# Moving the layer-input projection of an encoder block from its last stage to the end of its mixer

## The chip, the cores and the metric

The kernel runs on one core of a Trainium2 chip. The metric is the device time of one execution, in microseconds (us). Before the change it is 963.14 us, the median of three runs (962.81 to 963.81). About 0.2% of it, 1.9 us, can be told from no change.

A core has five engines, each with its own queue of instructions that it takes in order: TensorE (PE in the profile) for matmuls, with its weight loads shown apart (PEld); VectorE (DVE); ScalarE (ACT); GpSimd (POOL); and SyncE (SP), which here only issues DMAs. SBUF holds the working tiles of 128 partitions, PSUM the results of matmuls in eight banks.

## The reference, cut to what matters

One layer, 512 frames of width 1024, all in float32. `_swiglu`, `_conv_module` and `_gla` are the usual ones: a gated feed-forward block, a causal depthwise convolution of width 31 with layer norm over 512 channels, and a gated linear attention with four heads.

```
h = x
h = h + 0.5 * _swiglu(_rmsnorm(h, ffn1_norm[i]), ffn1_w_in[i], ffn1_w_out[i])
z = _rmsnorm(h, mix_norm[i]) @ w_in[i]
conv_a, conv_gt, q, k, v, r, g_lr = jnp.split(z, SPLIT_POINTS, axis=-1)
y_conv = _conv_module(conv_a, conv_gt, conv_w[i], conv_b[i], conv_ln_g[i], conv_ln_b[i])
y_gla = _gla(q, k, v, r, g_lr, gate_w_up[i], gate_b[i], gla_norm[i])
h = h + jnp.concatenate([y_conv, y_gla], axis=-1) @ w_out[i]
h = h + 0.5 * _swiglu(_rmsnorm(h, ffn2_norm[i]), ffn2_w_in[i], ffn2_w_out[i])
gate = jax.nn.sigmoid(_rmsnorm(h, ple_norm[i]) @ ple_w_gate[i])
h = h + gate * (p[i] @ ple_w_proj[i])
return _rmsnorm(h, final_norm)
```

The projection of the title is `p[i] @ ple_w_proj[i]`: p is 512 x 256, the weight 256 x 1024. It depends on nothing that the layer computes.

## The kernel before

**Precision.** A float32 product is made of three matmuls: each operand is split into a rounded high part and the low rest, and high x high, high x low and low x high are added in PSUM (`mm3`, line 209). The high part is a copy on ScalarE (`high`, line 183, and `high4`, line 219, which puts a weight into four smaller tiles), the low part a subtraction on VectorE (`low`, line 193). `added` (line 198) makes the low part otherwise: ScalarE writes the negated weight, and a DMA issued by GpSimd adds the weight to it. `ahead` (line 214) has GpSimd do the subtractions.

**Tiles.** `bt` hands out 41 tiles of 128 x 512 (tag A), `raw` six buffers for loaded weights, the tags wh and wl six each for their parts, `tmp("u1")` two, `bank` seven PSUM banks and `aux` one. An instruction that needs a tile waits until one is free.

**Order.** `Ordered` (lines 36 to 60) chains the instructions of PE, DVE and ACT in the order of the program text, from `in_order(True)` to `in_order(False)` at line 1446; this is why nearly every instruction is recorded under line 46. POOL and SP are not chained: the framework queues them by its own model of when each can start. In the last stage no engine is chained.

**Stages.** The first feed-forward block (up to about 363 us in the profile) is driven by a list of units with due times (`drive`, line 575): weights are fetched and split a fixed number of units ahead, and hooks run behind named units. Its last cut of the output product is done in pieces (`second`, line 742): first and second halves of four output pairs. The hook ("m4", 10) loads four tiles of the input projection and splits them at once (line 875).

The mixer follows. `zblock` (line 233) makes 128 x 512 blocks of the input projection, `tokblock` (line 1089) blocks of 128 tokens for v and r. The convolution is 124 VectorE steps, 31 for each of four channel groups, that `taps(n)` (line 905) puts between other work, always from the first two unfinished groups in turn; a call that finds a group finished is spent on removing it. `rsqrt_mean` (line 243) makes a root with a power on GpSimd, `spread` and `colsum` are small matmuls.

In the mixer's end (lines 1249 to 1416) the four blocks of r are made, gated with the attention's output (`ytok`), transposed into `yps`, split into `mix[4..7]` (ygH, ygL), and multiplied with the lower half of each of the eight output weights (`first_part`, line 1244). Between these stand four matmuls with a constant matrix (`mean`) that sum the convolution's four groups; then come the layer norm's squares, its root (`ln_sums`, a hook inside the half block of weight 3), its spreading and the norm itself (`ln_out`, a hook inside the half block of weight 6), which give `mix[0..3]` (ycH, ycL). The upper halves of the output weights follow, for weights 0 to 2 together, then one by one (`wout_h`, line 1361, takes each result into h).

The second feed-forward block is like the first (to about 894 us); `turn_p` (line 1395), which transposes and splits p, is hooked into its last units. In the last stage (lines 1451 to 1520), for each half e of the width and each token block t, six matmuls make the projection, ScalarE copies it out, four transposes bring h back to tokens, 24 matmuls make the gate, and `gated` combines them; the second half also normalises and stores.

Of the kernel before, what the change touches and what calls it, by code (L numbers as in the profile page):

```python
# [15 lines left out]
P = 128  # L16
SEQ = 512
# [45 lines left out]
def block_kernel(ctx: ExitStack, tc: tile.TileContext, a: dict, out: bass.AP):  # L63
# [11 lines left out]
    tp = ctx.enter_context(tc.tile_pool(name="tmp", bufs=2))  # L75
    pp = ctx.enter_context(tc.tile_pool(name="ps", bufs=8, space=PSUM))
# [137 lines left out]
    def ahead(src, c0, ncol):  # L214


        return [[low(w, pool) for w in high4(load(src, 0, DC, c, P))] for c in range(c0, c0 + ncol, P)]
# [377 lines left out]
    def ffn(w_in, w_out, x, gname, given, first, rsb, hooks, plain):  # L595
# [146 lines left out]
        def second(cut):  # L742
# [62 lines left out]
            if not last:  # L805
                return [piece(n, 0, True, True, ("g2", f0) if n == 0 else None) for n in range(0, DC, 2)]
            return ([piece(n, 0, True, False) for n in range(0, 6, 2)],
                    [piece(n, 1, False, True) for n in range(0, 6, 2)] + [piece(6, 0, True, False),
# [54 lines left out]
    w_ahead = []  # L863

    def sums_hooks(x, names, at):

        h = {}
        for name, key in zip(names, at):
# [6 lines left out]
                  ("m4", 10): lambda *_: w_ahead.extend([ahead(w_in, D_CONV, 2 * P), ahead(w_in, 0, 2 * P)])})  # L875
# [15 lines left out]
    glu, acc, conv = [], [cvt() for _ in range(4)], []  # L891
# [11 lines left out]
    turn = [0]  # L903

    def taps(n):

        for _ in range(n):
            if not conv:
                return
            i = turn[0] % min(2, len(conv))  # L910
            turn[0] += 1
            try:
                next(conv[i])
            except StopIteration:
                conv.pop(i)
# [13 lines left out]
    def glu_out(a1, sg):  # L929
# [3 lines left out]
        conv.append(conv_steps(len(glu) - 1))  # L933
# [33 lines left out]
    wq = [high(raw_q[0])]  # L967
    taps(2)
    low(wq[0])
    taps(1)  # L970
# [11 lines left out]
    wq.append(high(raw_q[1]))  # L982
# [24 lines left out]
    wk = [high(raw_k[0])]  # L1007
    low(wq[1])
    raw_v = [load(w_in, k, 2, C_V, SEQ) for k in (0, 2)]
    cums, epos, eneg, edec, decay, ends = [], [], [], [], [], []  # L1010
    taps(8)
    glu_out(glu_value(pa), sg)
    pb = zblock(w2b[1], hg)
    taps(3)
    low(wk[0])
# [18 lines left out]
    wk.append(high(raw_k[1]))  # L1034
# [29 lines left out]
    low(wk[1])  # L1064
# [3 lines left out]
    taps(5)  # L1068
# [181 lines left out]
    wo, rt = {n: added(ohigh(n)) for n in (0, 1)}, []  # L1250
    for t in range(TB):
# [5 lines left out]
        elif t == 1:  # L1257
            ps = tokblock(wr, t, {2: lambda: outputs(1)})
            taps(15)
# [7 lines left out]
        else:  # L1267
            ps = tokblock(wr, t)
# [14 lines left out]
        if t > 0:  # L1283
            taps((0, 2, 5, 3)[t])
# [3 lines left out]
    mub = aux()  # L1288
    for t in range(TB):
        if t == 2:  # L1290
            for c in range(2):
                pe.matmul(mub, mean, acc[c], start=(c == 0), stop=False)
        for h in range(4):
            pe.transpose(yps[h][:, t * P:(t + 1) * P], ytok[t][:, h * HV:(h + 1) * HV], ident)
    taps(2)
# [3 lines left out]
    wo[3] = ohigh(3)  # L1299
# [3 lines left out]
    pbt = [bt(s="ptok") for _ in range(2)]  # L1303
    ptok = [pbt[t // 2][:, (t % 2) * D_PLE:(t % 2 + 1) * D_PLE] for t in range(TB)]
# [4 lines left out]
    for steps in list(conv):  # L1309
        for _ in steps:  # L1310
            pass
# [232 lines left out]
```

## Time and profile before

| | |
|---|---|
| runs | 963.81, 962.81, 963.14 us |
| profiled execution | 963.15 us, its span from first to last instruction 961.4 us |
| instructions | 14302 |
| TensorE clock granted | 0.999 |
| VectorE, ScalarE, GpSimd busy | 72%, 52%, 4% of the span |
| DMA | 99.15 MB, mean 103 GB/s |

Times are microseconds from the start of the span. "Waits" list, for an engine, the tile that it was about to write or read, who released it, the total, the number of times and the longest. A timeline row is a start, a duration, the engine, and what is written from what; several like instructions in a row are merged (x4), and idle time before the row stands behind it with its releaser. The chain of waits is the chain of work that ended last. A stretch (busy time by windows) has the pairs PE, PEld, DVE, ACT, POOL as busy time and count, then the granted clock, the DMA share and GB/s.

### The profile page before, as it was taken

How to read it: one execution, taken by the hardware profiler on the slowest of the kernel's cores; microseconds unless marked ns; L12 is line 12 of the kernel's file. 1: busy time of each engine (PE TensorE's matmuls, PEld its weight loads, DVE VectorE, ACT ScalarE, POOL GpSimd, SP SyncE). 2: the span in 40 equal slices, each digit the busy share in tenths (PEclk: the TensorE clock that was granted, in tenths of full speed). 3: DMA queues.
4: the chain of work that ended last, by engine and by line, in shares of the span. 5: the costliest groups of instructions: out<-in, count | busy, mean ns of one | idle time of the engine just before them, and what ended most of it. 6: DMA issues, size and time to landing. Idle time of an engine off the chain costs nothing.

```text
span 961.4 us, 14302 instructions
## 1 busy us (share of the span) xinstructions
PE 947.4 (99%) x5809; PEld 838.4 (87%) x5809; DVE 693.6 (72%) x912; ACT 504.4 (52%) x795; POOL 38.8 (4%) x49
## 2 busy tenths in 40 slices
PE   8999999999999999999999999999999999999996
PEld 7888999999999978788877888999999999998885
DVE  4885767677677585999987679866776766767554
ACT  4854655554554453463564646556545555546442
POOL 0000000000000310001120000000000000000000
PEclk9999999999999999999999999999999999999999
DMA  8441323343223561125543232432243223334102
GB/s 244 140 130 64 104 72 112 109 131 93 84 88 110 153 175 50 39 85 136 132 96 102 75 101 66 132 98 80 88 132 110 82 92 113 96 125 153 45 1 88
DMA packets 102854, 99.15 MB, mean 103 GB/s; under 512 B 4499, under 2 KB 95717, under 8 KB 102788
## 3 DMA queue, kind: packets, MB, share of 16 engines
q1 hardware_dynamic: 100916, 94.05, 31.9%
q0 software_dynamic: 1296, 3.67, 2.2%
q8 instruction: 45, 0.74, 0.3%
q10 hardware_dynamic: 576, 0.52, 0.2%
q14 instruction: 21, 0.17, 0.1%
HBM read 92.46 MB, written 2.10 MB: 98 GB/s over the span
## 4 chain that ended last, share of the span: by engine, by line
PE 95%; DMA 1%; DVE 1%; ACT 1%; issue 1%; POOL 0%; SPq 0%; POOLq 0%; DVEq 0%; ACTq 0%
PE ps L46 94%; PE ax L46 1%; DMA wr<-in_w_in 1%; DMA x<-in_x 0%; DVE wl L46 0%; ACT wh L46 0%; POOL wa L46 0%; ACT wa L46 0%; DVE g L46 0%; ACT yc L46 0%; DVE ygL L46 0%; DVE actL L46 0%; DVE yc L46 0%; ACT ygH L46 0%; POOLq L1540 0%
## 5 line engine op out<-in xcount | busy, mean ns | idle before, releaser
L46 DVE TENSOR_TENSOR wl<-wr,wh 128x1024 fp32r<-128x1024 f32 (+2 forms) x181 | 214.3, 1195 | 76.1 <-ACT wh L46 75.7
L46 PE MATMUL ps<-hgH,wh 128*128 128x256 f32 (+1 forms) x768 | 239.6, 317 | 0.0
L46 PE MATMUL ps<-hgH,wl 128*128 128x256 f32 (+1 forms) x768 | 238.0, 315 | 0.0
L46 PE MATMUL ps<-hgL,wh 128*128 128x256 f32 (+1 forms) x768 | 237.9, 315 | 0.0
L46 ACT CAST wh<-wr 128x1024 fp32r<-128x1024 f32 (+2 forms) x186 | 187.4, 1024 | 40.0 <-PE ps L46 20.2
L46 PEld LDWEIGHTS ps<-hgH,wh 128*128 128x128 f32 x768 | 146.3, 191 | 11.7 <-ACT hgH L46 2.0
L46 PEld LDWEIGHTS ps<-hgL,wh 128*128 128x128 f32 x768 | 147.0, 191 | 9.8
L46 PEld LDWEIGHTS ps<-hgH,wl 128*128 128x128 f32 x768 | 145.9, 191 | 8.3
L46 PE MATMUL ps<-actH,wh 128*128 128x512 f32 x352 | 137.6, 391 | 1.2 <-ACT actH L46 1.2
L46 PE MATMUL ps<-actL,wh 128*128 128x512 f32 x352 | 137.5, 391 | 0.2 <-DVE actL L46 0.2
L46 PE MATMUL ps<-actH,wl 128*128 128x512 f32 x352 | 137.0, 389 | 0.0
L46 ACT ACTIVATE h<-ps 128x512 f32<-128x512 f32 x64 | 38.1, 595 | 115.1 <-PE ps L46 115.1
L46 DVE SCALAR_TENSOR_TENSOR cv<-glu,cw,cv 128x504 f32<-128x504 f32 (+25 forms) x120 | 81.2, 729 | 0.6
L46 PEld LDWEIGHTS ps<-actH,wh 128*128 128x128 f32 x352 | 66.2, 188 | 14.5 <-ACT actH L46 1.6
L46 ACT ACTIVATE s<-g 128x512 f32<-128x512 f32 x48 | 30.2, 629 | 91.4 <-DVE g L46 91.4
L46 PEld LDWEIGHTS ps<-actH,wl 128*128 128x128 f32 x352 | 66.1, 188 | 13.9
L46 PEld LDWEIGHTS ps<-actL,wh 128*128 128x128 f32 x352 | 66.2, 188 | 13.1 <-DVE actL L46 0.5
L46 DVE TENSOR_TENSOR actL<-m,actH 128x512 fp32r<-128x512 f32 x44 | 28.7, 689 | 43.1 <-ACT actH L46 42.9
L46 PE MATMUL ps<-wh,hgH 128*128 128x512 f32 (+1 forms) x136 | 52.4, 385 | 0.0
L46 PE MATMUL ps<-wl,hgH 128*128 128x512 f32 (+1 forms) x136 | 51.7, 380 | 0.0
L46 PE MATMUL ps<-wh,hgL 128*128 128x512 f32 (+1 forms) x136 | 51.3, 377 | 0.0
L46 DVE TENSOR_TENSOR wl<-sm,wh 128x1024 fp32r<-128x1024 f32 x34 | 41.4, 1218 | 10.1 <-ACT wh L46 10.1
(227 smaller groups left out, 1618.4 us busy)
## 6 DMA issues: line engine op xcount, KB each, us to landing
wr<-in_ffn_w_in SPq DMA_DIRECT2D x84, 512.0 KB
wr<-in_ffn_w_out SPq DMA_DIRECT2D x32, 512.0 KB
wr<-in_w_in SPq DMA_DIRECT2D x20, 512.0 KB
wr<-in_ffn_w_out SPq DMA_DIRECT2D x16, 384.0 KB
wr<-in_w_out SPq DMA_DIRECT2D x8, 512.0 KB
wr<-in_ple_w_gate SPq DMA_DIRECT2D x8, 512.0 KB
wl<-wr POOLq DMA_DIRECT2D x5, 512.0 KB, 5.6
x<-in_x SPq DMA_DIRECT2D x8, 256.0 KB
```

Source lines behind the costliest of these rows:

```text
L46: inst = call(*args, **kwargs)
```

## The change

The projection's eight groups (two halves of the width, four token blocks) are made in the mixer's end by a new function `project` and stored to a DRAM tile; the last stage loads each group back into the tile where ScalarE's copy went before. The tokens of p are loaded, transposed (inside the third r block) and split in the mixer, and the projection's weight is split into tag-A tiles with `added`. Two groups stand ahead of the first half block, one behind the third, three behind the layer norm's column sums, two behind its spreading.

The four mean products become one, over the sum of the four groups that VectorE makes; the half blocks of weights 3, 6 and 7 are done after the joint loop of weights 0 to 2, in the order 0, 1, 2, 4, 5, 3, 6, 7, and these three weights are split after the layer norm.

`taps` now takes the group with the most steps left, never the same one twice in a row if another is ready, and no call is spent on removal. The weights of q and k are split with `added`, with more convolution steps in place of the subtractions. The four tiles of the input projection that were split at once behind ("m4", 10) are now only loaded there; they are split behind two pieces of the output product (new keys ("p", 4) and ("p", 0)).

The diff, cut to its changed lines:

```diff
@@ -73,6 +73,7 @@
+    dp = ctx.enter_context(tc.tile_pool(name="spill", bufs=1, space=bass.MemoryType.DRAM))
@@ -211,10 +212,9 @@
-    def ahead(src, c0, ncol):
-        return [[low(w, pool) for w in high4(load(src, 0, DC, c, P))] for c in range(c0, c0 + ncol, P)]
+    def ahead(raws):
+        return [[low(w, pool) for w in high4(r3)] for r3 in raws]
@@ -804,8 +804,8 @@
-            return ([piece(n, 0, True, False) for n in range(0, 6, 2)],
-                    [piece(n, 1, False, True) for n in range(0, 6, 2)] + [piece(6, 0, True, False),
+            return ([piece(n, 0, True, False, ("p", n) if n else None) for n in range(0, 6, 2)],
+                    [piece(n, 1, False, True, None if n else ("p", n)) for n in range(0, 6, 2)] + [piece(6, 0, True, False),
@@ -860,7 +860,7 @@
-    w_ahead = []
+    w_ahead, raw_ahead = [], []
@@ -872,7 +872,9 @@
-                  ("m4", 10): lambda *_: w_ahead.extend([ahead(w_in, D_CONV, 2 * P), ahead(w_in, 0, 2 * P)])})
+                  ("m4", 10): lambda *_: raw_ahead.extend(load(w_in, 0, DC, c, P) for c in (D_CONV, D_CONV + P, 0, P)),
+                  ("p", 4): lambda *_: w_ahead.append(ahead(raw_ahead[:2])),
+                  ("p", 0): lambda *_: w_ahead.append(ahead(raw_ahead[2:]))})
@@ -888,7 +890,7 @@
-    glu, acc, conv = [], [cvt() for _ in range(4)], []
+    glu, acc, conv, steps_of = [], [cvt() for _ in range(4)], [], {}
@@ -900,19 +902,20 @@
-    turn = [0]
+    left = {}
...
-            i = turn[0] % min(2, len(conv))
-            turn[0] += 1
-            try:
-                next(conv[i])
-            except StopIteration:
-                conv.pop(i)
+            ready = conv[:2] if len(glu) < 4 or len(conv) > 3 else conv
+            c = max((c for c in ready if c != left.get("last") or len(ready) == 1), key=lambda c: left[c])
+            next(steps_of[c])
+            left["last"] = c
+            left[c] -= 1
+            if not left[c]:
+                conv.remove(c)
@@ -930,7 +933,9 @@
-        conv.append(conv_steps(len(glu) - 1))
+        c = len(glu) - 1
+        conv.append(c)
+        left[c], steps_of[c] = PAD + 1, conv_steps(c)
@@ -964,10 +969,8 @@
-    wq = [high(raw_q[0])]
-    taps(2)
-    low(wq[0])
-    taps(1)
+    wq = [added(high(raw_q[0]))]
+    taps(4)
@@ -979,7 +982,7 @@
-    wq.append(high(raw_q[1]))
+    wq.append(added(high(raw_q[1])))
@@ -1004,15 +1007,13 @@
-    wk = [high(raw_k[0])]
-    low(wq[1])
+    wk = [added(high(raw_k[0]))]
...
-    taps(8)
+    taps(10)
...
-    taps(3)
-    low(wk[0])
+    taps(5)
@@ -1031,7 +1032,7 @@
-    wk.append(high(raw_k[1]))
+    wk.append(added(high(raw_k[1])))
@@ -1061,11 +1062,10 @@
-    low(wk[1])
...
-    taps(5)
+    taps(7)
@@ -1248,6 +1248,47 @@
+    w_proj, pT, lowers = a["ple_w_proj"][0], [], []
+    proj = dp.tile([TB, 2, P, SEQ], F32, name="proj")
+    pbt = [bt(s="ptok") for _ in range(2)]
+    ptok = [pbt[t // 2][:, (t % 2) * D_PLE:(t % 2 + 1) * D_PLE] for t in range(TB)]
+    for t in range(TB):
+        nc.sync.dma_start(out=ptok[t], in_=a["p"][0, 0, t * P:(t + 1) * P, :])
+    def turn_p(k):
+        ps = bank()
+        for t in range(TB):
+            pe.transpose(ps[:, t * P:(t + 1) * P], ptok[t][:, k * P:(k + 1) * P], ident)
+        hi, lo = bt(F32R, "pTH"), bt(F32R, "pTL")
+        act.copy(hi, ps)
+        pT.append((hi, lo))
+        lowers.append(lambda: dve.tensor_tensor(out=lo, in0=ps, in1=hi.bitcast(F32), op=ALU.subtract))
+    wp_ = {}
+    def high_p(e):
+        r3 = load(w_proj, 0, 2, e * SEQ, SEQ)
+        wp_[e] = []
+        for k in range(2):
+            hi, lo = bt(F32R, "wpH"), bt(F32R, "wpL")
+            act.copy(hi, r3[:, k])
+            wp_[e].append(added((hi, lo, r3[:, k])))
+    def project(e, t):
+        ps = bank()
+        ts = slice(t * P, (t + 1) * P)
+        for k in range(2):
+            xh, xl = pT[k]
+            wh, wl, _ = wp_[e][k]
+            pe.matmul(ps, xh[:, ts], wh, start=(k == 0), stop=False)
+            pe.matmul(ps, xl[:, ts], wh, start=False, stop=False)
+            pe.matmul(ps, xh[:, ts], wl, start=False, stop=(k == 1))
+        o = bt(s="pq")
+        act.copy(o, ps)
+        nc.sync.dma_start(out=proj[t, e], in_=o)
@@ -1256,6 +1297,7 @@
+            high_p(0)
@@ -1265,7 +1307,9 @@
-            ps = tokblock(wr, t)
+            ps = tokblock(wr, t, {8: lambda: turn_p(0), 16: lambda: turn_p(1)} if t == 2 else {})
+            if t == 2:
+                high_p(1)
@@ -1281,82 +1325,75 @@
-            taps((0, 2, 5, 3)[t])
+            taps((0, 2, 5, 0)[t])
+            for f in lowers if t == 3 else ():
+                f()
...
-    mub = aux()
...
-        if t == 2:
-            for c in range(2):
-                pe.matmul(mub, mean, acc[c], start=(c == 0), stop=False)
...
-    taps(2)
+    taps(1)
...
-    wo[3] = ohigh(3)
...
-    pbt = [bt(s="ptok") for _ in range(2)]
-    ptok = [pbt[t // 2][:, (t % 2) * D_PLE:(t % 2 + 1) * D_PLE] for t in range(TB)]
-    for t in range(TB):
-        nc.sync.dma_start(out=ptok[t], in_=a["p"][0, 0, t * P:(t + 1) * P, :])
+    project(0, 0)
+    project(0, 1)
...
-    for steps in list(conv):
-        for _ in steps:
-            pass
-    conv.clear()
-    low(wo[3])
+    while conv:
+        taps(1)
...
-    pe.matmul(mub, mean, acc[2], start=False, stop=False)
-    first_part(5, wo[5])
-    pe.matmul(mub, mean, acc[3], start=False, stop=True)
-    first_part(2, wo[2])
-    sqs, lln, yc = [], [], []
+    project(0, 2)
+    total = bt(s="total")
+    for c in range(1, 4):
+        dve.tensor_tensor(out=total, in0=total if c > 1 else acc[0], in1=acc[c], op=ALU.add)
+    mub = aux()
+    pe.matmul(mub, mean, total, start=True, stop=True)
+    sqs, yc = [], []
...
-    for n in (6, 7):
-        wo[n] = ohigh(n)
+    first_part(5, wo[5])
+    first_part(2, wo[2])
...
-    def ln_sums():
-        lln.append(rsqrt_mean(colsum([sqs[0]]), D_CONV, TB, between=lambda: low(wo[6])))
-    def ln_out():
-        rln = spread(lln[0], copy=False)
-        for c in range(5):
-            if c < 4:
-                t, hi, lo = bt(s="yc"), bt(F32R, "ycH"), bt(F32R, "ycL")
-                dve.tensor_tensor(out=t, in0=acc[c], in1=rln, op=ALU.mult)
-                act.activation(t, t, AF.Silu, bias=vec("conv_ln_b", c), scale=vec("conv_ln_g", c))
-                act.copy(hi, t)
-                mix[c] = hi, lo
-                yc.append(t)
-            if c:
-                hi, lo = mix[c - 1]
-                dve.tensor_tensor(out=lo, in0=yc[c - 1], in1=hi.bitcast(F32), op=ALU.subtract)
-        low(wo[7])
-    first_part(3, wo[3], {7: ln_sums})
-    first_part(6, wo[6], {7: ln_out})
+    lln = rsqrt_mean(colsum([sqs[0]]), D_CONV, TB)
+    project(0, 3)
+    project(1, 0)
+    project(1, 1)
+    rln = spread(lln, copy=False)
+    for c in range(5):
+        if c < 4:
+            t, hi, lo = bt(s="yc"), bt(F32R, "ycH"), bt(F32R, "ycL")
+            dve.tensor_tensor(out=t, in0=acc[c], in1=rln, op=ALU.mult)
+            act.activation(t, t, AF.Silu, bias=vec("conv_ln_b", c), scale=vec("conv_ln_g", c))
+            act.copy(hi, t)
+            mix[c] = hi, lo
+            yc.append(t)
+        if c:
+            hi, lo = mix[c - 1]
+            dve.tensor_tensor(out=lo, in0=yc[c - 1], in1=hi.bitcast(F32), op=ALU.subtract)
+    project(1, 2)
+    project(1, 3)
+    for n in (3, 6, 7):
+        wo[n] = ohigh(n)
+        low(wo[n])
...
-    nhg, later, squares = [], [], []
+    nhg, later, squares = [None] * DC, [], []
@@ -1371,7 +1408,7 @@
-            nhg.append((hi, lo))
+            nhg[n] = hi, lo
@@ -1390,24 +1427,12 @@
-    pT = []
-    def turn_p(k):
-        ps = aux()
-        for t in range(TB):
-            pe.transpose(ps[:, t * P:(t + 1) * P], ptok[t][:, k * P:(k + 1) * P], ident)
-        hi, lo = bt(F32R, "pTH"), bt(F32R, "pTL")
-        act.copy(hi, ps)
-        dve.tensor_tensor(out=lo, in0=ps, in1=hi.bitcast(F32), op=ALU.subtract)
-        pT.append((hi, lo))
-    for n in range(7):
+    for n in (0, 1, 2, 4, 5, 3, 6, 7):
+        if n in (3, 6, 7):
+            first_part(n, wo[n])
...
-    first_part(7, wo[7])
-    part(half[7][1], half[7][0], range(0, 4), False, True)
-    wout_h(7, half[7][1])
@@ -1441,7 +1466,6 @@
-    hooks.update({("m7", 10): lambda *_: turn_p(0), ("m5", 10): lambda *_: turn_p(1)})
@@ -1466,18 +1490,11 @@
-        wph, wpl = parts(load(a["ple_w_proj"][0], 0, 2, e * SEQ, SEQ))
...
-            pt, pq = bank(), bank()
-            for k in range(2):
-                xh, xl = pT[k]
-                pe.matmul(pq, xh[:, ts], wph[:, k, :], start=(k == 0), stop=False)
-                pe.matmul(pq, xl[:, ts], wph[:, k, :], start=False, stop=False)
-                pe.matmul(pq, xh[:, ts], wpl[:, k, :], start=False, stop=(k == 1))
-            ppr = tmp("u1")
-            act.copy(ppr, pq)
+            pt, ppr = bank(), tmp("u1")
+            nc.sync.dma_start(out=ppr, in_=proj[t, e])
```

## The prediction

> **What bounds the kernel now.** I read the page first (span and busy time), then the waits of TensorE, the chain of waits, the busy time by stretch, and the timelines of the engines around the edits.
>
> ```profile
> span 961.4 us, 14302 instructions
> PE 947.4 (99%) x5809; PEld 838.4 (87%) x5809; DVE 693.6 (72%) x912; ACT 504.4 (52%) x795; POOL 38.8 (4%) x49
> ```
> TensorE is busy 947.4 of 961.4 us. A change can therefore gain only by taking instructions from TensorE or by filling its idle time; work that is merely moved from one place on it to another is worth nothing. The idle time is 14 us, and the waits say which of it belongs to the stretches touched:
>
> ```profile
> PE ps L46 <- ACT ycH L46: 1.6, 1, 1.6
> PE ps L46 <- ACT actH L46: 1.2, 1, 1.2
> ...
> PE ps L46 <- ACT ygH L46: 0.5, 1, 0.5
> PE ps L46 <- DVE ygL L46: 0.3, 1, 0.3
> PE ps L46 <- DVE actL L46: 0.2, 1, 0.2
> ```
> ycH is the convolution's normalised output, ygH/ygL the attention's, actH/actL the last activations of the first feed-forward stage. Together 3.8 us. The rest lies at the two ends of the program, which the edits leave alone.
>
> **Part by part.** First the price of a projection group and of a mean product, from TensorE's timeline in the last stage and the chain of waits in the mixer's end:
>
> ```profile
> 894.15 0.39 PE L46 MATMUL ps<-wh,pTH 128*128 128x512 f32 x1
> ...
> 895.51 0.60 PE L46 MATMUL ps<-ident,h 128*128 128x128 f32 x4
> ```
> ```profile
> 504.92 0.86 PE ax L46 x2
> 505.77 2.74 PE ps L46 x12
> ```
> Six matmuls of the projection take 895.51 - 894.15 = 1.36 us, 0.23 from start to start, though each record is 0.39 long; so matmuls are priced by their starts. Twelve (half an output block) take 2.74.
>
> *Projection.* Eight groups leave the last stage: -8 x 1.36 = -10.9 us, on the path, since TensorE has no wait there. The same eight enter the mixer's end: +10.9. The two transposing steps move from the second feed-forward stage to the mixer, equally at nothing. By itself the move is zero; its worth is the waits that the groups cover.
>
> *Mean.* Four products become one: -3 x 0.86 = -2.6 us of TensorE. The three additions that replace them are VectorE's.
>
> *Waits.* A wait is counted from the modelled end of the matmul before it, 0.16 later than the next would have started (0.39 - 0.23). The five waits thus stand for 3.8 + 5 x 0.16 = 4.6 us. Do the groups cover them, and what is late next?
>
> - ycH: after the spreading product comes 2 x 1.36 = 2.7 us of projection. In the chain, from that product's end to ycH:
>
> ```profile
> 515.23 0.04 DVE ms L46
> ...
> 518.48 1.03 PE ax L46 x8
> ...
> 519.54 0.70 DVE yc L46
> ...
> 520.26 0.82 ACT yc L46
> ...
> 521.11 0.63 ACT ycH L46
> ```
> 521.74 - 519.51 = 2.2 us: covered, with 0.5 to spare. The root before it gets three groups, 4.1 us, and took 518.48 - 515.23 = 3.3 here.
> - ygH and ygL: two groups, 2.7 us, stand ahead of the first output block; see the new wait below.
> - actH and actL: ScalarE stood waiting for the input projection's weights just ahead of the activations' split:
>
> ```profile
> ACT wa L46 <- DMA wr<-in_w_in: 6.5, 4, 2.9
> ```
> ```profile
> 329.67 5.28 DMA wr<-in_w_in
> ```
> The change keeps these loads and moves the conversion behind the next pieces of the output product, so ScalarE is not blocked: both waits go.
>
> *The mean's own chain.* The one product needs all four channels, then nothing but two half blocks (2 x 2.74 = 5.5 us) covers subtraction, squares and sums. Before:
>
> ```profile
> 498.51 9.22 DVE L46 SCALAR_TENSOR_TENSOR cv<-glu,cw,cv 128x510 f32<-128x510 f32 x12
> ...
> 509.41 2.48 DVE L46 TENSOR_TENSOR cv<-cv,ax 128x512 f32<-128x512 f32 x4 [0.56 <-PE ax L46]
> 511.81 2.28 DVE L46 TENSOR_TENSOR lnsq<-lnsq,lnsq 128x512 f32<-128x512 f32 x3
> ```
> 514.1 - 509.4 = 4.7 us, so 0.8 is left. Counted from the end of the last token block, 491.8, twelve steps ended at 507.7, 15.9 later. After the change 7 steps are left there (the calls add up to 117 of 124, against 112): 7 x 0.65 on alternate channels instead of 12 x 0.77 on one is 4.6 instead of 9.2, and one conversion less is queued ahead. They end near 11 after that block, the three additions (2.28 for such three) near 13; TensorE reaches the product after the transposes, two groups, three half blocks and a group, 1.8 + 2.7 + 8.2 + 1.4 = 14. Free, by 1 us.
>
> *VectorE.* It is saturated here (busy time by stretch; VectorE has 19.73 of 20.00, ScalarE 11.87):
>
> ```profile
> 460.00:480.00 20.00, 20.00 (x155) 16.61 (x154) 19.73 (x38) 11.87 (x40) 3.10 (x3) 1.00 0.66 159
> ```
> Four conversions of q and k leave it for ScalarE and an accumulating DMA, and 8 more steps come before the heads' root:
>
> ```profile
> 461.17 1.22 DVE L46 TENSOR_TENSOR wl<-wr,wh 128x1024 fp32r<-128x1024 f32 x1
> ...
> 468.18 9.73 DVE L46 SCALAR_TENSOR_TENSOR cv<-glu,cw,cv 128x494 f32<-128x494 f32 x15
> ...
> 478.15 0.18 DVE L46 TENSOR_TENSOR so<-so,rs 128x16 f32<-128x16 f32 x1 [0.24 <-ACT sq L46]
> ```
> With a step at 9.73/15 = 0.65, 8 x 0.65 - 4 x 1.22 = +0.3; the 0.24 of waiting takes most of it, but conversions overlap a little, so the root comes 0 to 0.4 late. ScalarE has room for the q and k halves.
>
> *The new wait.* ScalarE's queue, in program order: scaled outputs, two pT copies, four wp instructions, r(2), four of wo[4], r(3). Queued behind all of it: the product of y(3), then TensorE's last four transposes.
>
> ```profile
> 483.05 4.25 ACT L46 ACTIVATE y<-ps,rs 128x128 f32<-128x128 f32 x16 [1.24 <-DVE rs L46]
> 487.07 0.81 ACT L46 ACTIVATE r<-ps,rs 128x512 f32<-128x512 f32 x1
> 487.64 1.26 ACT L46 CAST wa<-wr 128x512 fp32r<-128x512 f32 x2
> 488.67 1.28 ACT L46 ACTIVATE wa<-wr 128x512 fp32r<-128x512 f32 x2
> 492.00 0.69 ACT L46 ACTIVATE r<-ps,rs 128x512 f32<-128x512 f32 x1 [2.05 <-PE ps L46]
> ```
> ```profile
> 491.80 1.03 PE L46 MATMUL ps<-ident,y 128*128 128x128 f32 x8
> ```
> Six instructions at 0.52 each put r(2) at 490.2, r(3) at 492.8, and with 0.69 for it and, as an estimate, as much for the product of y(3) the transposes at 494.2. TensorE, with eight transposes (0.9 by their starts) put into the block, has done twelve more at 491.8 + 0.9 + 1.3 = 494.0. With the root's 0 to 0.4 and two hand-overs that is 0.3 to 1.0 us of waiting; I take 0.8. At best it is nothing; at worst see the first rival.
>
> *Rest.* The stores and reloads of the projection go on SP's queue. A reload needs its buffer, freed by the product two blocks earlier, and has a block and a half to land: nothing on the path. The three late weights (3, 6, 7) have the 8 us of the first joint loop: nothing.
>
> Sum against the profiled execution (963.15, 0.01 from the median of the runs): -2.6 - 4.6 + 0.8 = -6.4, so **956.8 us**.
>
> **A rule that speaks against it.** The eight GpSimd subtractions of the input weights now fall beside a busier VectorE. The rows:
>
> ```profile
> 324.34 0.69 DVE L46 TENSOR_TENSOR u<-u,bc 128x512 f32<-128x512 f32 x1
> ...
> 330.70 1.74 DVE L46 TENSOR_TENSOR u<-u,bc 128x512 f32<-128x512 f32 x1
> ```
> ```profile
> 345.00:362.00 17.00, 17.00 (x77) 14.05 (x76) 14.92 (x22) 9.92 (x15) 0.53 (x1) 1.00 0.57 149
> ```
> The same instruction takes 1.05 more while GpSimd subtracts. Eight times 1.05 is 8.4 us; VectorE has 2.1 idle in the new place, so up to 6.3 could be left at the mixer's start, where the last halves of the normalised input are needed after 21 matmuls, 4.8 us: 1.5 us of waiting at worst. I take nothing, since the first four run before the crowded part. [...]
>
> **Rivals.**
> *1. GpSimd's queue.* The heads' root and the new accumulating DMAs share it. If the two DMAs of the first projection weight stand ahead of the root, it starts 2 to 2.5 us later, and the chain through y, r(2), r(3) has no slack: 956.8 + 2.5 = 959.3.
>
> ```profile
> 466.21 0.86 POOL L46 DMA_DIRECT2D wl<-wr  x1 [24.92 <-DVE cv L46]
> ...
> 478.62 3.34 POOL L46 TENSOR_TENSOR rs<-ms,negh 128x16 f32<-128x16 f32 x1 [9.66 <-DVE ms L46]
> ```
> Against it: ScalarE's last square ends just ahead of the 478.15 quoted above, and a copy and a negation, 0.52 each, come before the first DMA: 479.2, half a microsecond behind the root's 478.62. 17%.
> *2. Two-input contention*, as above: 958.3. 8%.
> *3. The waits only move.* ScalarE carries twelve more half conversions and eight evictions; if each covered wait comes back elsewhere, the mean's 2.6 is all that stays: 960.6. For it: every slack above is about 1 us. 9%.
> *4. Slower: reloads behind stores.* In the last four blocks, reload t+1 could be queued on SP behind the output store of block t:
>
> ```profile
> 932.43 0.69 DVE L46 TENSOR_TENSOR s<-s,u 128x512 f32<-128x512 f32 x1 [4.33 <-ACT s L46]
> ...
> 936.83 0.54 DVE L46 TENSOR_SCALAR y<-g,rs,rs 128x512 f32<-128x512 f32 x1
> ```
> ```profile
> 889.78 0.89 SPq L1453 DMA_DIRECT2D gfin<-in_final_norm  x2
> ```
> A block would then last 4.9 plus the load L, against 5.9 of TensorE (24 matmuls 5.5, four transposes 0.4). Three such blocks cost 3 x (L - 1.0), so from L = 3.1 us the gain is gone. L is between nothing and the 5.28 of the 512 KB load: up to 956.8 + 12.8 = 969.6, and 965.2 at L = 3.8, which I take as nearer to the whole than to half the bytes. Against it: SP's order is not the program's; the final gain, written ahead of the gate's weights, went out last, at 889.78. 11%. [...]
>
> **Numbers.** The forecast has 55%, with its own range 955.2 (no new wait, and some 0.1 saved at each change of matmul kind) to 958.0. The range to 961.0 takes in rivals 1 to 3. About 0.2% (1.9 us) can be told from no change: faster means under 961.2, which holds in the forecast and rivals 1 to 3 but for a little of the third: 0.85; same 0.08 and slower 0.07 from the fourth and what I have not seen.
>
> **What would show it.** Right: TensorE's waits without ycH, actH and actL; one pair of mean records; the last stage 10.9 shorter; the first joint loop starting some 1 to 1.5 earlier than 521.8. Wrong: a wait of over 2 us on y or ygH (rival 1), on hgL at the mixer's start (rival 2), on the product of all four channels (my 1 us was too short), or reload rows of SP after 930 that follow the stores (rival 4).

## The result, and the profile after the change

The changed kernel takes 955.96 us (median of four executions, 955.52 to 956.18), against 963.47 for the kernel before in the same comparison. The ratio is 0.992, with a 95% interval of 0.9903 to 0.9938: a gain of 7.5 us where 6.4 was forecast. The profiled execution took 955.52.

The head of the page after the change:

```profile
span 953.8 us, 14362 instructions
PE 941.9 (99%) x5803; PEld 837.1 (88%) x5803; DVE 687.6 (72%) x909; ACT 509.7 (53%) x805; POOL 46.1 (5%) x57
```
TensorE has six instructions fewer: three mean products, each recorded twice. It is busy 5.5 us less, and idle 11.9 instead of 14.0. Of the 5.5, the three products are 2.6, the start of the program about 0.9; the rest, as an estimate by subtraction, are matmuls that had run long beside the old waits. These are all its waits (engine, tile, who released it: total, times, longest):

```profile
PE ax L46 <- POOL ident masks.py:199: 1.6, 1, 1.6
PE ps L46 <- DMA x<-in_x: 1.3, 1, 1.3
PE ps L46 <- DVE y L46: 0.7, 1, 0.7
```
The first two are the start of the program. The waits on ycH, ygH, ygL, actH and actL are gone; the third row is the new wait that the prediction expected, forecast at 0.8 and measured at 0.69. Its chain, on ScalarE, then VectorE, then TensorE:

```profile
488.11 0.82 ACT L46 ACTIVATE r<-ps,rs 128x512 f32<-128x512 f32 x1
488.68 1.28 ACT L46 CAST wa<-wr 128x512 fp32r<-128x512 f32 x2
489.71 1.29 ACT L46 ACTIVATE wa<-wr 128x512 fp32r<-128x512 f32 x2
490.76 0.82 ACT L46 ACTIVATE r<-ps,rs 128x512 f32<-128x512 f32 x1
```
```profile
491.61 0.69 DVE L46 TENSOR_TENSOR y<-y,r 128x512 f32<-128x512 f32 x1 [0.76 <-ACT r L46]
```
```profile
490.20 1.47 PE L46 MATMUL ps<-ident,y 128*128 128x128 f32 x12
492.36 0.66 PE L46 MATMUL ps<-ident,y 128*128 128x128 f32 x4 [0.69 <-DVE y L46]
```
Here r(t) is the block of r for token block t, and y(t) its product with the attention's output. ScalarE runs without a gap from r(2) to r(3), so r(3) starts 0.56 behind the end of its block at 490.20, where it was 0.20 before (492.00 against 491.80).

The single mean product, on VectorE and TensorE:

```profile
501.53 0.69 DVE L46 TENSOR_TENSOR total<-cv,cv 128x512 f32<-128x512 f32 x1
502.25 1.42 DVE L46 TENSOR_TENSOR total<-total,cv 128x512 f32<-128x512 f32 x2
```
```profile
505.14 1.02 PE L46 MATMUL ax<-total,mean 128*128 128x512 f32 x2
...
520.13 0.39 PE L46 MATMUL ps<-ycH,wh 128*128 128x512 f32 x1
```
The sum is ready at 503.67, 1.5 us ahead of the product (forecast: 1). The joint loop starts at 520.13 instead of 521.78. At the end, the first transposes of the first and the last block of the last stage, and the last matmul:

```profile
896.94 0.60 PE L46 MATMUL ps<-ident,h 128*128 128x128 f32 x4
...
939.20 0.60 PE L46 MATMUL ps<-ident,h 128*128 128x128 f32 x4
...
945.26 0.28 PE L46 MATMUL ps<-wl,hgH 128*128 128x256 f32 x1
```
Seven blocks take 42.26 us. Before they took 51.91 (from 895.51 to 947.42), so 9.65 less; with the group that stood ahead of the first transposes (1.36) that is 11.0 for the eight groups, which were priced at 10.9.

The same places of TensorE's timeline in all kernels, from one profiled execution each:

| kernel | mixer's first matmul | joint loop | between | last matmul | span | behind it |
|---|---|---|---|---|---|---|
| before | 363.27 | 521.78 | 158.51 | 953.48 | 961.4 | 7.9 |
| after | 360.72 | 520.13 | 159.41 | 945.26 | 953.8 | 8.5 |
| mean_only | 362.73 | 522.42 | 159.69 | 954.11 | 962.0 | 7.9 |
| ahead_only | 360.38 | 518.90 | 158.52 | 950.63 | 958.5 | 7.9 |
| projection_only | 362.79 | 524.79 | 162.00 | 949.92 | 958.5 | 8.6 |
| dealing_only | 362.08 | 520.67 | 158.59 | 952.40 | 960.3 | 7.9 |
| projection_back | 360.58 | 516.11 | 155.53 | 955.43 | 963.4 | 8.0 |
| dealing_undone | 360.73 | 523.17 | 162.44 | 948.30 | 956.9 | 8.6 |
| sp_in_order | 360.65 | 520.09 | 159.44 | 945.26 | 961.8 | 16.5 |
| root_behind | 361.34 | 522.75 | 161.41 | 947.88 | 956.4 | 8.5 |
| wp_late | 361.61 | 522.01 | 160.40 | 947.19 | 955.7 | 8.5 |
| fill_y | 361.82 | 521.17 | 159.35 | 946.35 | 954.9 | 8.6 |
| both | 361.99 | 521.32 | 159.33 | 946.45 | 954.4 | 8.0 |
| dummy_fill | 361.09 | 515.78 | 154.69 | 952.93 | 960.9 | 8.0 |

The first column is not a matter of these edits alone: "after", the eight kernels made from it and ahead_only are equal up to there, and yet it lies between 360.38 and 361.99. Differences below 1.6 us are therefore read from "between" and "behind it", not from the whole time. "Between" holds different work in different kernels: two half blocks (of weights 3 and 6) in before, mean_only, ahead_only and dealing_only, the projection's groups in after and the others that have them there, neither in projection_back and dummy_fill. It is compared only within such a group. Each ratio below is to the kernel before, on the same chip; the three rounds of experiments ran on three chips.

### The profile page after: what moved, and what is told of

It is laid out like the page before. It is cut to its first block, busy times and chain, and to the rows that moved or that the text cites. A ratio compares the mean times of both kernels' runs of the same rounds, so it can differ in the third digit from the quotient of the medians.

```text
span 953.8 us, 14362 instructions
## 1 busy us (share of the span) xinstructions
PE 941.9 (99%) x5803; PEld 837.1 (88%) x5803; DVE 687.6 (72%) x909; ACT 509.7 (53%) x805; POOL 46.1 (5%) x57
## 4 chain that ended last, share of the span: by engine, by line
PE 93%; DVE 2%; issue 1%; ACT 1%; POOL 1%; DMA 0%; POOLq 0%; DVEq 0%; SPq 0%; ACTq 0%
PE ps L46 92%; PE ax L46 1%; DVE cv L46 1%; POOL rs L46 0%; DMA x<-in_x 0%; ACT y L46 0%; DVE wl L46 0%; DVE st L46 0%; DVE g L46 0%; DVE y L46 0%; DVE sc L46 0%; ACT sq L46 0%; DVE rs L46 0%; ACT wa L46 0%; DVE s L46 0%
## 5 line engine op out<-in xcount | busy, mean ns | idle before, releaser
L46 DVE TENSOR_TENSOR wl<-wr,wh 128x1024 fp32r<-128x1024 f32 (+2 forms) x175 | 207.0, 1195 | 73.2 <-ACT wh L46 73.0
L46 DVE SCALAR_TENSOR_TENSOR cv<-glu,cw,cv 128x482 f32<-128x482 f32 (+29 forms) x120 | 80.2, 727 | 0.3
```

The lines of the kernel that those rows point to most:

```text
L46: inst = call(*args, **kwargs)
```

## Experiments: the four parts alone

Theory: TensorE sets the time; the projection's worth is that its groups fill waits, the mean's that three products go, and the even dealing is what lets the single product be on time. Rival: each edit has its gain of its own, and they add up.

**mean_only** (from before). The edit:

```diff
-        if t == 2:
-            for c in range(2):
-                pe.matmul(mub, mean, acc[c], start=(c == 0), stop=False)
...
     conv.clear()
+    total = bt(s="total")
+    for c in range(1, 4):
+        dve.tensor_tensor(out=total, in0=total if c > 1 else acc[0], in1=acc[c], op=ALU.add)
...
-    pe.matmul(mub, mean, acc[2], start=False, stop=False)
     first_part(5, wo[5])
-    pe.matmul(mub, mean, acc[3], start=False, stop=True)
+    pe.matmul(mub, mean, total, start=True, stop=True)
```


> From the kernel before, only the mean: the four groups of the convolution are added up on VectorE and one product stands where the fourth stood. Theory A (the single product has no room without the rest of the change): in the kernel before the convolution ends at 507.7 and three additions take 2.1 to 2.3 more, while TensorE, with three products fewer, would be there at about 507; a wait of about 2.5 us on total appears, the transposes of the last y lose the two products that covered them, and the time is 964.4 (963.5 to 965). Theory B (three products of 0.86 are simply gone, as the prediction's term counts them): 960.6.

Measured: 963.93, ratio 1.0006 (0.9997 to 1.0015), and 1.18 more between mixer and joint loop. Theory A's sum holds: three products fewer, and nothing gained. Its inside doesn't: the wait on total is 0.6, not 2.5. TensorE's timeline shows why:

```profile
494.86 0.50 PE L46 MATMUL ps<-ygH,wh 128*128 128x512 f32 x1 [1.27 <-ACT ygH L46]
495.64 0.50 PE L46 MATMUL ps<-ygL,wh 128*128 128x512 f32 x1 [0.29 <-DVE ygL L46]
...
496.71 0.63 PE L46 MATMUL ps<-ygH,wl 128*128 128x512 f32 x1
497.14 0.63 PE L46 MATMUL ps<-ygH,wh 128*128 128x512 f32 x1
```
The two products had stood between the transposes. Without them the wait on ygH grows from 0.5 to 1.3, and behind it, from 496.71 on, matmuls start 0.43 apart instead of 0.23. The granted clock is 0.92 in the mean of 480 to 500 us, and 1.00 in the kernel before: as an estimate from these two, half the clock for some 3 us. TensorE came late by itself, so it waited less for total.

**ahead_only** (from before): the `ahead`, ("p", n) and ("m4", 10) lines of the change's diff, and nothing else.

> From the kernel before, only the input projection's weights: loaded at the same place, converted behind two pieces of the output product. Theory A: the two waits actH and actL go, 1.4 us and 0.16 for each, and nothing comes back: 961.3 (961.0 to 961.5). Theory B (GpSimd's subtractions beside a busier VectorE): the gain is eaten by a wait on hgL at the mixer's start of up to 1.5: 962.8 to 963.1.

Measured: 961.08, ratio 0.9977 (0.9968 to 0.9987); actH and actL are gone from the waits, and none on hgL has come. Theory A.

**projection_only**. The projection's part of the diff alone; the third and later groups stand here:

```diff
     first_part(2, wo[2])
+    project(0, 2)
...
     lln = rsqrt_mean(colsum([sqs[0]]), D_CONV, TB)
+    project(0, 3)
+    project(1, 0)
+    project(1, 1)
     rln = spread(lln, copy=False)
```


> From the kernel before, only the projection (stored in the mixer, loaded back, with the half blocks of weights 3, 6 and 7 late, as the eight groups need the PSUM banks); four mean products, the old dealing of the steps and the old place of the input weights. Third and fourth group stand behind the third half block's successors instead of ahead of the mean. Theory A: the waits on ycH, ygH and ygL go (1.7 and 1.1 us), about 0.8 of small halts around the column sums too, a wait of about 0.6 on the squares appears, and the end of the program is 0.6 longer as in the changed kernel: 960.7 (960 to 961.5). Theory B (waits only move): within 0.5 of 963.1.

Measured: 960.09, ratio 0.9968 (0.9955 to 0.998). The waits on ycH, ygH and ygL are gone, one of 0.7 on the squares has come (forecast 0.6), and the end is 0.7 longer. Theory A.

**dealing_only** (from before): the `taps`, `left` and `added(high(raw_q...))` lines of the diff.

> From the kernel before, only the convolution's steps dealt evenly, with q's and k's low parts made by an accumulating DMA. Theory A: by itself it is worth nothing, since no wait of TensorE in the kernel before hangs on the convolution's end: 963.1 within 0.5. Theory B (VectorE is full here, so freeing it moves the waits on yg and ycH): 962 or less.

Measured: 963.46, ratio 1.0 (0.9991 to 1.0009); 158.59 between mixer and joint loop, where it was 158.51. Theory A: worth nothing alone.

Alone, the four parts change the median by +0.8, -2.1, -3.1 and +0.3, together -4.1. The whole change gives -7.5. So the parts don't add up; the next runs show which two belong together.

## Experiments: one part undone, and two rivals made on purpose

**dealing_undone** (from after): the old `taps` and counts, and q's and k's low parts on VectorE again.

> From the changed kernel, only the convolution's dealing undone (old order of steps, q's and k's low parts on VectorE). Theory A: 12 steps of 0.77 instead of 7 of 0.65 are left behind the last block of r, the convolution ends 4.5 later, 1.5 of that is slack, and a wait of 3.0 on total appears: 958.7 (958 to 959.2). Theory B (the single product has room anyway): 955.7.

Measured: 958.79, ratio 0.9961 (0.9949 to 0.9973), 3.03 more between mixer and joint loop. VectorE's last steps, behind which the sum of the groups starts at 505.86, and TensorE:

```profile
496.72 9.22 DVE L46 SCALAR_TENSOR_TENSOR cv<-glu,cw,cv 128x510 f32<-128x510 f32 x12
```
```profile
508.05 1.13 PE L46 MATMUL ax<-total,mean 128*128 128x512 f32 x2 [2.21 <-DVE total L46]
```
Theory A: twelve steps on one channel group, and a wait of 2.2 on total; the wait on y grows to 1.2 besides. This part is worth nothing that can be told alone, and 3 us where one product waits for all four groups. The run takes back the even dealing and the low parts of q and k together; which of the two counts for how much, it does not tell.

**projection_back** (from after): the eight groups and p's transposes in the last stages, as before the change.

```diff
-    project(0, 0)
-    project(0, 1)
     first_part(0, wo[0])
...
-    project(0, 3)
-    project(1, 0)
-    project(1, 1)
     rln = spread(lln, copy=False)
...
-            nc.sync.dma_start(out=ppr, in_=proj[t, e])
+            for k in range(2):
+                xh, xl = pT[k]
+                pe.matmul(pq, xh[:, ts], wph[:, k, :], start=(k == 0), stop=False)
...
+            act.copy(ppr, pq)
```


> From the changed kernel, only the projection undone: its eight groups and p's transposes stand in the last stages again, everything else as changed. Theory A (the groups' worth is that they cover waits): about 1.3 us on ygH and ygL, 0.7 on the sum of the four channels, 2.3 to 3.2 on the root's spreading, 2.2 on ycH come back, less the 0.85 of the wait on y that halves and the 0.6 at the program's end: 962.5 (961.5 to 963.5). Theory B (the gain is the mean's three products and the first stage's two waits, and half blocks cover the rest): 958 or less.

Measured: 965.52, ratio 1.0023 (1.0014 to 1.0033): slower than before the change, and 9.6 slower than with the groups. Theory A, but 3 us more than its sum. The waits are as forecast (2.3 on the root, 2.3 on ycH, 1.3 and 0.3 on yg, 0.2 on y), but for the 0.7 on the sum of the four channels, which TensorE reached too late to wait for. Behind two of them the clock falls again:

```profile
512.70 1.13 PE L46 MATMUL ax<-ident,rs 128*128 128x128 f32 x8 [2.25 <-DVE rs L46]
516.11 0.80 PE L46 MATMUL ps<-ycH,wh 128*128 128x512 f32 x1 [2.28 <-ACT ycH L46]
516.70 0.63 PE L46 MATMUL ps<-ycH,wl 128*128 128x512 f32 x1
517.13 0.63 PE L46 MATMUL ps<-ycH,wh 128*128 128x512 f32 x1
```
Busy time by stretch; the third number from the right is the granted clock:

```profile
480.00:500.00 20.00, 18.24 (x79) 14.55 (x79) 15.84 (x29) 13.87 (x32) 4.42 (x5) 0.91 0.52 109
500.00:520.00 20.00, 15.47 (x66) 12.46 (x65) 11.86 (x23) 7.72 (x12) 1.03 (x1) 0.85 0.27 76
```
The half blocks of weights 3 and 6, which stood between these waits before the change, are behind the joint loop here, as in the changed kernel. A kernel with the other three parts and these two half blocks in their old place was not run. So 9.6 us is what the groups are worth in the changed order; against the best order without them it may be less.

**dummy_fill** (from projection_back): matmuls that nobody reads (`dummy(n, ps, x)` multiplies one weight tile with x, n times), shorter than the waits they stand in.

```diff
+    dummy(5, aux(), hg[0][0])
     first_part(0, wo[0])
...
+    dummy(9, bank(), mix[4][0])
     rln = spread(lln, copy=False)
...
+    dummy(9, bank(), mix[4][0])
     for n in (3, 6, 7):
```


> The kernel with the projection undone (965.5), with 23 matmuls whose results nobody reads put into three waits: 5 ahead of the first half block, 9 ahead of the root's spreading, 9 behind it, each set shorter than its wait. Theory A (the loss beyond the waits is the granted clock, which fell to half for 8 matmuls behind the wait on yg and 10 behind that on ycH, 0.2 each): full clock throughout, 965.5 - 3.6 = 961.9, with the waits shorter by the dummies and the joint loop starting as late as its data allow. Theory B (the loss lies elsewhere): 965.5 or more.

Measured: 962.95, ratio 1.0 (0.9991 to 1.0008), where projection_back had 1.0023: about 2.2 us faster by the ratios, 2.6 by the medians, with 23 matmuls more. The same two stretches:

```profile
480.00:500.00 20.00, 19.40 (x92) 15.48 (x91) 15.65 (x29) 13.86 (x32) 4.78 (x6) 1.00 0.48 97
500.00:520.00 20.00, 19.28 (x90) 14.91 (x88) 12.41 (x24) 7.96 (x13) 1.03 (x1) 1.00 0.32 88
```
Theory A: the clock stays full. It does so in every execution: the granted clock of the whole program is 0.997 to 0.999 in all eleven, and was 0.990 to 0.994 in all nine of projection_back. From mixer to last matmul the profile has 3.0 less (591.84 against 594.85), not 3.6, since TensorE is now early at the mean product and waits 0.5 for total. Of the groups' 9.6 us, 2.2 to 3.0 are thus kept clock, and about 7 covered waits.

**sp_in_order** (from after): SyncE's loads and stores of the last half in program order.

```diff
+        sp.on, sp.last = e == 1, None
         for t in range(TB):
...
-            nc.sync.dma_start(out=ppr, in_=proj[t, e])
+            sp.dma_start(out=ppr, in_=proj[t, e])
...
-                nc.sync.dma_start(out=out[0, ts, i * SEQ:(i + 1) * SEQ], in_=y)
+                sp.dma_start(out=out[0, ts, i * SEQ:(i + 1) * SEQ], in_=y)
```


> From the changed kernel, SyncE's queue of the last half kept in the order of the program text, so that the reload of block t+1 stands behind the stores of block t: the prediction's fourth rival, made on purpose. Theory A (its formula, 3 x (L - 1.0), with L near the 3.7 from issue to landing of the 256 KB accumulating DMAs): 955.7 + 8.1 = 963.8, and 960.5 at L = 2.6. Theory B (a reload is quick beside a block): within 0.5 of 955.7.

Measured: 963.73, ratio 1.0005 (0.9996 to 1.0013): the fourth rival would have cost the whole gain. SyncE's queue, then VectorE:

```profile
932.84 0.81 SPq L46 DMA_DIRECT2D out<-y  x2
933.75 0.40 SPq L46 DMA_DIRECT2D u<-proj  x1
```
```profile
936.83 0.69 DVE L46 TENSOR_TENSOR s<-s,u 128x512 f32<-128x512 f32 x1 [3.56 <-DMA u<-proj]
...
945.37 0.69 DVE L46 TENSOR_TENSOR s<-s,u 128x512 f32<-128x512 f32 x1 [3.54 <-DMA u<-proj]
```
A reload takes 3.1 us from issue to use, and VectorE's blocks are 8.54 apart. That the time came out at Theory A's sum is luck: the formula's L of 3.7 was 0.6 too long, and its 4.9 for the rest of a block 0.5 too short, since 5.4 us pass from the addition at 936.83 to the issue of the next reload. TensorE loses nothing: its last matmul starts at 945.26 as in the changed kernel, and the whole loss stands behind it (16.5 against 8.5). In the changed kernel the reloads don't stand behind the stores of the block before:

```profile
908.77 20.56 SPq L1497 DMA_DIRECT2D u<-proj  x5
932.86 0.81 SPq L1537 DMA_DIRECT2D out<-y  x2
934.92 0.33 SPq L1497 DMA_DIRECT2D u<-proj  x1
```
The last one, at 934.92, does follow two stores, but these are of the first of the four blocks, three back; VectorE uses it at 943.99 and doesn't wait for it.

**root_behind** (from after): the first weight's two DMAs chained ahead of the heads' root on GpSimd.

```diff
+            pool.on, pool.last = True, None
             high_p(0)
...
+            pool.on = False
```


> From the changed kernel, only GpSimd's order: the two DMAs of the first projection weight ahead of the heads' root, the prediction's first rival made on purpose. ScalarE has the halves ready at 476.5 and 477.6, so the root starts near 478.5 instead of 476.6. Theory A (the chain root, y, r(2), r(3), y(3) has no slack): the wait on y grows from 0.7 to 2.6, 957.6 (the prediction's price of 2.5 would give 958.2). Theory B (there is slack in ScalarE's queue): 955.7 within 0.4.

Measured: 957.6, ratio 0.9945 (0.9933 to 0.9956), 2.00 more between mixer and joint loop; the wait on y is 2.0. Theory A, at the price of this experiment's sum; the prediction had 2 to 2.5 and took the upper end.

## Experiments: can the new wait and the longer end be had back?

**wp_late** (from after):

```diff
-            if t == 2:
-                high_p(1)
...
+        if t == 3:
+            high_p(1)
         if t > 1:
```


> From the changed kernel, only the second projection weight's four ScalarE instructions moved from ahead of r(2) to behind r(3). Theory A (the prediction's: ScalarE's queue makes the wait on y): the wait of 0.69 goes, 955.1. Theory B (the chain block of r, r(3), y(3), transposes is longer than the twelve transposes by itself): r(3) can start 0.2 behind the block's end instead of 0.56, so 0.36 of the wait goes and 0.3 stays: 955.6.

Measured: 957.17, ratio 0.9941 (0.9929 to 0.9954), and 0.99 more between mixer and joint loop: neither theory. The wait on y falls to 0.2, as far as it can by r(3)'s own chain; but ScalarE's four instructions now stand ahead of ygH, and TensorE waits there:

```profile
496.77 0.50 PE L46 MATMUL ps<-ygH,wh 128*128 128x512 f32 x1 [0.58 <-ACT ygH L46]
497.55 0.50 PE L46 MATMUL ps<-ygL,wh 128*128 128x512 f32 x1 [0.28 <-DVE ygL L46]
```
**fill_y** (from after):

```diff
     for t in range(TB):
+        if t == 3:
+            project(0, 0)
         for h in range(4):
...
-    project(0, 0)
     project(0, 1)
```


> From the changed kernel, only the first projection group (1.36 us of TensorE) moved ahead of the last four transposes of y. Theory A: it covers the wait on y, and the one group that is left covers ygH and ygL, which had 0.7 to 1.1 to spare: 955.1, no wait on y, yg or total. Theory B (waits only move): a wait on ygL or on total of the same size appears, 955.9.

Measured: 956.03, ratio 0.9927 (0.9913 to 0.994). The wait on y is gone; the table has 159.35 against 159.41. Theory B: what TensorE saves at y it loses behind it, with a wait of 0.2 on ygL and slower starts around it. ScalarE holds ygH, since it runs without a gap up to it and now evicts the group first:

```profile
493.47 1.31 ACT L46 ACTIVATE wa<-wr 128x512 fp32r<-128x512 f32 x2
494.53 0.73 ACT L46 COPY pq<-ps 128x512 f32<-128x512 f32 x1
494.99 2.58 ACT L46 ACTIVATE ygH<-ps,vcol 128x512 fp32r<-128x512 f32 x4
```
So ScalarE's queue from the scaled outputs to ygH is the bound of this stretch, and an order that only shifts work within it gains nothing. Moving the conversion of `wo[5]` behind ygH would shorten it; that was not tried.

**both** (fill_y, and the two output products of the block before the last held back until the last block's first half is added; from there on VectorE is chained in program order):

```diff
                 gated(ps, rs[:, t:t + 1], ppr[:, cs], pt[:, cs], hn[:, cs], ss)
+                while held:
+                    held.pop(0)()
```


> The changed kernel with fill_y and one more edit: in the last stage the two output products of the block before the last stand on VectorE behind the last block's first half, not ahead of its addition. Theory A (the longer end of the program comes from those two instructions, 0.9 us ahead of the addition that ScalarE's square, and behind it the last sigmoid, wait for): the last sigmoid starts 0.05 behind the last matmul instead of 0.56, and with fill_y the time is 954.6. Theory B (the end is as long as before by other waits): as fill_y, 955.1.

Measured: 955.93, ratio 0.9925 (0.9913 to 0.9937); 8.0 behind the last matmul instead of 8.6. The last sigmoid, in the changed kernel and in this one:

```profile
946.16 0.45 ACT L46 ACTIVATE s<-ps,rs 128x256 f32<-128x256 f32 x1
```
```profile
946.77 0.47 ACT L46 ACTIVATE s<-ps,rs 128x256 f32<-128x256 f32 x1
```
It starts 0.90 behind the start of the last matmul (945.26) there, 0.32 behind it (946.45) here. Theory A for the end, by the profile; 0.6 us is too little for the ratio to show. No version beat the changed kernel by more than can be told.

## Why the prediction was right, point by point

- **The move itself at zero.** Right: 11.0 left the last stage, and by their starts the groups cost 11.3 in the mixer. Its worth is cover: 3.1 us alone in the kernel before, and undone in the changed kernel it takes back more than the whole gain.
- **Mean, -2.6.** Right as far as the runs go: no wait on the sum has come, with the slack that the text gave it (1.5, forecast 1). dealing_undone shows that 3.0 would come back without the other dealing, and mean_only that the same edit alone gains nothing. The prediction saw the condition. No run puts the three products back into the changed kernel, so the 2.6 itself is a price, not a measurement.
- **actH and actL.** 1.4 and two times 0.16 were forecast, 1.7; 2.0 was gained. From a small matmul near 112 us to the mixer's first, every one of the ten kernels with this edit takes 248.5, and the four without take 250.4 to 250.5. That matmul, before and after:

```profile
112.75 0.25 PE L46 MATMUL ax<-ident,vcolr 42*128 42x42 f32 x1
```
```profile
112.23 0.25 PE L46 MATMUL ax<-ident,vcolr 42*128 42x42 f32 x1
```
So of the 2.55 between the two first profiles 0.5 is start-up. The 0.3 that the forecast lacked is the matmuls behind the two waits, which start 0.73 and 0.34 apart instead of 0.23 (kernel before):

```profile
342.89 0.50 PE L46 MATMUL ps<-actH,wh 128*128 128x512 f32 x1 [1.21 <-ACT actH L46]
343.62 0.50 PE L46 MATMUL ps<-actL,wh 128*128 128x512 f32 x1 [0.23 <-DVE actL L46]
343.96 0.39 PE L46 MATMUL ps<-actH,wl 128*128 128x512 f32 x1
```
- **ycH, ygH, ygL, and the new wait.** All three gone, as forecast; 0.69 on y for 0.8. The heads' root came 0.55 later behind the mixer's start than in the kernel before, where 0 to 0.4 was forecast. ScalarE's queue does make the wait, but only 0.5 of it: r(3)'s own chain leaves 0.2 (wp_late).
- **Not forecast, a gain.** From mixer to last matmul 5.67 is gained (590.21 against 584.54), where the mean, three waits and the new one make 4.7. The column sums and the spreading stood inside half blocks, and matmuls around them started late, by too little for the list of waits. Together with these late starts they cost 2.65 before and 1.80 after, which is most of the 1.0; why the matmuls were late, the profile does not say. In the kernel before:

```profile
516.07 0.40 PE L46 MATMUL ps<-ygL,wh 128*128 128x512 f32 x1
516.59 0.50 PE L46 MATMUL ps<-ygH,wl 128*128 128x512 f32 x1
```
These two are 0.52 apart instead of 0.23. The prediction had put such gains into the range, not into the sum.
- **Not forecast, a loss.** The end is 0.6 longer. With blocks 5.9 apart instead of 7.3, the last block's first half meets the output products of the block before on VectorE:

```profile
944.33 0.54 DVE L46 TENSOR_SCALAR y<-hf,rs,rs 128x512 f32<-128x512 f32 x1
944.79 0.54 DVE L46 TENSOR_SCALAR y<-g,rs,rs 128x512 f32<-128x512 f32 x1
945.24 0.41 DVE L46 TENSOR_TENSOR g<-ps,s 128x256 f32<-128x256 f32 x1
```
The prediction had called the two ends of the program untouched; "both" shows the two products as the cause.
- **The sum.** -6.4 forecast. In the two profiled executions 0.5 of start-up, 0.3 at actH and actL and 1.0 of small halts come on top, and 0.6 at the end is lost: -7.6, which is what they show (963.15 and 955.52). The terms were right in kind, and near in size. That the number came out within 1 us is in part luck: a gain and a loss that the sum did not have are of opposite sign, and the start-up is chance.
- **Rivals.** The first didn't occur, since GpSimd's root went ahead of the DMAs (476.62 against 479.95); it would have cost 2.0. The second had no price: VectorE is slowed beside GpSimd's subtractions (in the changed kernel a subtraction at 343.90 takes 1.77, the same at 346.39, without one beside it, 1.23), but TensorE did not wait for it (ahead_only). The third is wrong for the whole change and right for the small stretch behind y. The fourth would have cost 7.8; the prediction's 8.4 is near to it by two errors that cancel, an L of 3.8 for 3.1 and a block's rest of 4.9 for 5.4. The L of 2.6 that the expectation of sp_in_order sets beside 3.7 is shown by no run; its reload took 3.1. The rival didn't occur, as SyncE's queue is not in program order. Its sign, a reload row after 930 behind stores, is there once (934.92), but as a sign it was too wide: it did not ask whose stores they are.

## What to carry to other kernels

Work that depends on nothing is best kept as filler for the stretch where the busiest engine waits: here moving it was worth 3.1 us alone and 9.6 in the changed order, and its own length hardly played a part. Edits that are worth nothing alone can be the condition for others, so undoing one part from the finished version tells more than adding it alone. When a wait is covered, look who is next in the queue of the engine that made it: on ScalarE the wait on y and the wait on ygH were one and the same length of queue.

## What the runs showed of the hardware

A wait can cost more than its length. In projection_back, a wait of 1.27 and one of 0.29 behind four small transposes, and two waits of 2.25 and 2.28 with eight small matmuls between them, were each followed by matmuls at 0.43 instead of 0.23 from start to start, up to about 497 (the last slow one starts at 496.65) and up to 520.91: about 8 and 10 of them, some 3.6 us lost together by the profile, at a granted clock of 0.91 from 480 to 500 us and of 0.85 from 500 to 520. The two slow stretches lasted about 3.5 and 4.8 us; no wait ahead of them was longer than 2.3. A single wait of 2.21 in dealing_undone, with full matmuls on both sides, left the granted clock at 1.00 from 500 to 520 us, and behind the 1.6 on ycH in the kernel before matmuls start 0.23 to 0.24 apart from 522.11 on. 23 matmuls that nobody reads kept the clock at 1.00 (dummy_fill, 480 to 520 us). In root_behind a wait of 2.00 stands between twelve small transposes and four more, and the granted clock is 1.00 from 480 to 520 us:

```profile
494.98 0.66 PE L46 MATMUL ps<-ident,y 128*128 128x128 f32 x4 [2.00 <-DVE y L46]
```
So which waits bring the clock down stays open; the runs show that it happens, what it cost, and that in dummy_fill filling the waits prevented it.

The start of the program differs by more than most edits here are worth. Kernels equal up to the mixer reach it at 360.38 to 361.99. Between two of them, wp_late (361.61) and the changed kernel (360.72), 0.8 of the 0.9 is four of the first matmuls, which take 1.91 in the one and 1.09 in the other:

```profile
9.01 1.91 PE L46 MATMUL ps<-hgL,wh 128*128 128x512 f32 x4
```
```profile
9.00 1.09 PE L46 MATMUL ps<-hgL,wh 128*128 128x512 f32 x4
```
A difference of a microsecond is therefore better read from a matmul behind the start than from the whole time.
